# Products over 64 features issued for two heads by turns on the two partition halves

## The chip, the cores and the metric

One core of one Trainium2 chip runs the whole kernel. The metric is the device time in microseconds, the median of three runs. All operands are float32; the large weight products are split into two float32r parts each and done as three products.

## What is computed

Two blocks of a network over 256 tokens of 1024 features. The first block has two layers with a modulation by a condition vector: an even layer (a dilated-mixture attention of 8 heads and a differential attention of 4 heads with two maps each) and an odd layer (banded attention of 16 heads with sinks). The second block has two layers, each with four mixers (stick-breaking attention, an RWKV-7 recurrence, MoBA attention, HGRN2) of 4 heads each and a gated feed-forward part. Every head has 64 features, so the products between queries and keys, and those of the RWKV chunk matrices, contract over 64:

```python
s = jnp.einsum('bhqd,bhkd->bhqk', qs, k) * scale + bias        # attention scores, d = 64
z = jnp.einsum('bhtd,bhsd->bhts', qf[:, :, t0:kv_len], kf[:, :, :kv_len]) * scale   # stick-breaking
S_t = S_{t-1} diag(w_t) + (S_{t-1} a_t) b_t^T + v_t k_t^T ; y_t = S_t r_t           # RWKV, done in chunks of 128
```

## The kernel before

Queries and keys lie feature-major: a tile [128, 2, 256] holds two column tiles of 128 features, which are two heads each, one on partitions 0 to 63 and one on 64 to 127. A product of queries and keys of one head reads one half of the partitions and writes 128 queries by 128 or 256 keys into PSUM. There are two token tiles `t`.

PSUM has two pools of four banks: `mm` for the weight products (`proj_tok`, `proj_fm`, `proj_acc`, lines 237 to 239) and `mx` for everything else: scores (`sc`), values (`pv`), transposes (`pt`, `tr`), the sums of the modulation (`mod`) and all of the mixers' small tiles.

`softmax` (line 358) does the product itself (line 361), then on VectorE the biased minimum (line 363), then on ScalarE the exponential (line 366). It is called once for each head and token tile, so the product of the second token tile, into the same bank, follows in the program behind the VectorE read of the first. The callers are `scores_a` (8 heads, line 611), `scores_b` (4 heads with two maps, line 666), `scores` of the odd layer (16 heads, line 774) and `scores` of `moba` (4 heads, both layers, line 1035). `pipelined` runs the scores of a head two heads (one head of `scores_b`) ahead of its values: transposes (line 375), a copy to SBUF by ScalarE (line 377) and the products with the values (lines 637, 699, 805). In `moba` the scores of head h+1 are a step ahead of the values of head h.

`stick_breaking` (line 958) does for each token tile and each partition half two products of one half into one bank (line 971), then the sigmoid on ScalarE and, two steps later, the other half. `Rwkv.run` makes the chunk matrices (line 1346) for two chunks, two sources and two halves: two products of one half into one bank, then a mask by VectorE (line 1349).

The order on each engine is the planner's: it takes the ready instruction of the highest priority, priority being the program's order, which `lazily(by)` shifts. The odd layer's attention has -3000 and so goes before the weight products around it; the RWKV stream has -4000 against the stream of the other three mixers, with which `weave` mixes it step by step. Weight products fill the rest. The units of weights come by SyncE's queue (line 216), are rounded by ScalarE (line 219) and their rest taken by VectorE (line 220). In the even layer the same queue brings the modulation weights (line 482), which VectorE sums (lines 427 and 429), and the biases (line 381). `later` starts and ends such sums between the heads.

Of the kernel before, what the change touches and what calls it, by code (L numbers as in the profile page):

```python
# [94 lines left out]
NR, NH, NL = 3, 5, 5  # L95
LATE = 300


class Net:
# [109 lines left out]
    def unit(self, src, shape, pieces=1):  # L209
        """[128, 1024] weights: float32 in, split exactly into float32r parts."""  # L210
# [12 lines left out]
    def block(self, w, c0, k0=0, k1=8, pieces=1):  # L223
        """512 columns of w [1024, cols] as units of two k chunks; returns {chunk: (hi, lo)}."""
# [38 lines left out]
    def proj_fm_part(self, act, w, c0, done, k0, k1, ps, cols=4, wb=None):  # L263
        """cols * 128 columns, feature-major: done(i, ps) with ps [128, 2, 256] = column tiles 2i, 2i+1."""
# [43 lines left out]
    def to_T(self, src, t, act, c0, n):  # L308
        """transpose src [128 tokens of tile t, n*128] into chunks c0.. of act (hi, lo)."""
# [13 lines left out]
    def rstd(self, ss, n, eps, m=1):  # L323
        """(ss / n + eps) ** -0.5 for a [128, m] column block."""
# [7 lines left out]
    def norm_stat(self, t, junk):  # L332
        """rstd of token tile t (the squares by halves, times 1/32 squared = 1/D)"""
# [35 lines left out]
    def transpose_p(self, p, dst, evict):  # L369
        """p [128 q, t, 256 keys] -> dst [128 keys, kc, 256 q]"""  # L370
# [26 lines left out]
class Mod:  # L397
    """ada modulation of layer l, on every partition: norm_g * (1 + scale), shift, gate / 2."""

    def __init__(self, n, l):  # L400
        self.n, self.l = n, l
        self.G = n.s2(f"G{l}", tag="mod")
        if l == 0:
            # over the partitions by TensorE, idle as yet
# [43 lines left out]
    def start(self, half, then=None):  # L448
        """scale (first half: on TensorE, idle then) and shift (VectorE), before anything else runs"""
# [43 lines left out]
class AdaNorm:  # L493
    """rms_norm(x) * G + shift, by token tiles, transposed into act"""
# [15 lines left out]
def silu2(n, ps, out):  # L510
    """out = 2 silu(ps)"""
# [16 lines left out]
def pipelined(items, first, second, lag=2, after=None):  # L528
    """first(i) runs `lag` items ahead of second(i)"""
# [10 lines left out]
def pair_out(n, y, sg, col, yT, chunk):  # L540
    """y [128, t, 128] times the gates, into chunk `chunk` of yT"""
# [11 lines left out]
def even_layer(n, mod, later, follow):  # L553
# [24 lines left out]
    # the modulation and the normalized activations by halves of the features, products running along  # L578
# [31 lines left out]
    # dilated attention  # L610
    def scores_a(h):
        b = n.dma_bias(h)
        sp = v2(n.mx("sc"))
        p = v2(n.s2("p", tag="p"))
        rl = n.col(2, "rl")
        b0 = (h % 2) * 64
        for t in range(2):
            l, _ = n.softmax(sp[:, t, :], fm["qa", h // 4][b0:b0 + 64, h // 2 % 2, t * 128:t * 128 + 128],
                             fm["ka", h // 4][b0:b0 + 64, h // 2 % 2, :], b[:, t, :], p[:, t, :])
            nc.vector.reciprocal(rl[:, t:t + 1], l)  # L620
        return p, rl

    ya = {}
    st = {}

    def values_a(h, got):
        p, rl = got
        hh = h % 2
        if hh == 0:
            st["pv"] = n.mx("pv")  # L630
            ya[h // 2] = n.s2("ya", tag="yp").rearrange("p (t d) -> p t d", t=2)
        pv = st["pv"]
        pT = n.s2("pT", tag="pT")
        n.transpose_p(p, pT, nc.scalar.copy)
        for t in range(2):
            for kc in range(2):
                nc.tensor.matmul(pv[:, t * 128 + hh * 64:t * 128 + hh * 64 + 64],
                                 lhsT=pT[:, kc * 256 + t * 128:kc * 256 + t * 128 + 128],
                                 rhs=tok["va", kc][:, h * 64:h * 64 + 64], start=(kc == 0), stop=(kc == 1))
            c = slice(hh * 64, hh * 64 + 64)  # L640
            nc.scalar.activation(ya[h // 2][:, t, c], pv[:, t * 128 + hh * 64:t * 128 + hh * 64 + 64], AF.Copy,
                                 scale=rl[:, t:t + 1])
    pipelined(8, scores_a, values_a, 2, lambda h: later(h // 2) if h % 2 else None)
# [5 lines left out]
    # lambda, on every partition  # L649
# [15 lines left out]
    # differential attention  # L665
    def scores_b(h):
        b = n.dma_bias(8 + h)
        ps_, rs = [], []
        for m in range(2):
            sp = v2(n.mx("sc"))  # L670
            p = v2(n.s2("p", tag="p"))
            b0 = m * 64
            r = n.col(2, "rl")
            for t in range(2):
                l, _ = n.softmax(sp[:, t, :], fm["qb", h // 2][b0:b0 + 64, h % 2, t * 128:t * 128 + 128],
                                 fm["kb", h // 2][b0:b0 + 64, h % 2, :], b[:, t, :], p[:, t, :])
# [47 lines left out]
def odd_layer(n, act, mod, later, follow):  # L724
# [49 lines left out]
    def scores(h):  # L774
        g = h // 4
        b = n.dma_bias(12 + h)
        sp = v2(n.mx("sc"))
        p = v2(n.s2("p", tag="p"))
        den = n.col(4, "den")
        b0 = (h % 2) * 64  # L780
        for t in range(2):
            l, nm = n.softmax(sp[:, t, :], fm["q", h // 4][b0:b0 + 64, (h // 2) % 2, t * 128:t * 128 + 128],
                              fm["k", g % 2][b0:b0 + 64, g // 2, :], b[:, t, :], p[:, t, :],
                              init=sk[:, 16 + h:17 + h])
            nc.scalar.activation(den[:, 2 + t:3 + t], nm, AF.Exp, bias=sk[:, h:h + 1])
            nc.vector.tensor_add(den[:, t:t + 1], den[:, 2 + t:3 + t], l)
        nc.vector.reciprocal(den[:, 0:2], den[:, 0:2])
        return p, den

    yp = {}  # L790
    st = {}

    def values(h, got):
        p, den = got
        hh, g = h % 2, h // 4
        if hh == 0:
            st["pv"] = n.mx("pv")
            yp[h // 2] = n.s2("yc", tag="yp").rearrange("p (t d) -> p t d", t=2)
        pv = st["pv"]
        pT = n.s2("pT", tag="pT")  # L800
        n.transpose_p(p, pT, nc.scalar.copy)
        for t in range(2):
            o = pv[:, t * 128 + hh * 64:t * 128 + hh * 64 + 64]
            for kc in range(2):
                nc.tensor.matmul(o, lhsT=pT[:, kc * 256 + t * 128:kc * 256 + t * 128 + 128],  # L805
                                 rhs=tok[kc][:, g * 64:g * 64 + 64], start=(kc == 0), stop=(kc == 1))
            nc.vector.tensor_scalar(yp[h // 2][:, t, hh * 64:hh * 64 + 64], o, den[:, t:t + 1], None, op0=OP.mult)
# [5 lines left out]
    def after(h):  # L813
        if h in (1, 3, 5):
            later(h // 2)
        if h == 11:
# [10 lines left out]
def first_block(n):  # L827
# [14 lines left out]
    def later(i):  # L842
        """sums of part i; the part before it, complete by now, is spread over the partitions"""
# [12 lines left out]
class PlainNorm:  # L856
    """rms_norm(x) * g, by token tiles, transposed into act"""
# [13 lines left out]
class DoubleNorm:  # L871
    """x := rms_norm(x) * final_g, and the next norm of that, its sum of squares taken from x * final_g"""
# [9 lines left out]
    def tile(self, t):  # L882
# [10 lines left out]
        # 1 / r1^2 = m + eps with m the mean square of x; 1 / (r1 r2)^2 = mean square of y + eps (m + eps)  # L893
# [27 lines left out]
def weave(a, b):  # L921
    """steps of two independent instruction streams, by turns"""
# [7 lines left out]
def zsel(ap, b, z):  # L930
    """[P, m] -> [P, n, b]: every other run of b columns"""
# [3 lines left out]
def zsel4(ap, b, z):  # L935
    """[P, 4 * 128] -> [P, 4, n, b]"""
# [759 lines left out]
```

## Time and profile before

| | us |
|---|---|
| median of three runs | 1361.11 |
| lowest and highest run | 1355.42, 1362.63 |
| span of the profiled execution, first to last instruction | 1352.0 |
| TensorE (PE) busy in it | 1295.5 |
| VectorE (DVE) busy | 843.8 |
| ScalarE (ACT) busy | 647.7 |
| GpSimd (POOL) busy | 71.6 |

The profiled execution gives no time beside its span. Line numbers are those of the kernel before. A float32 matmul of the program stands in the trace as two records (two loads and two matmuls), each of which streams its columns twice. Busy times of PE count matmuls that overlap as one; a matmul's own duration holds its way through the array, so distances between starts or ends tell the pace.

### The profile page before, as it was taken

The page shows a single profiled execution, that of the slowest core. Times are in us where ns is not written, and L with a number is a line of the kernel's source. Part 1 is how long each engine was busy: PE and PEld are TensorE (multiplying, and loading weights), DVE is VectorE, ACT ScalarE, POOL GpSimd, SP SyncE. Part 2 cuts the span into 40 slices and gives each one's busy share as a digit, 9 for nine tenths or more (in the row PEclk, how much of TensorE's full clock was granted, in tenths as well). Part 3 has the DMA queues.
Part 4 walks back from the last instruction along what each step waited for, and adds up shares of the span by engine and source line. Part 5 has one row for each costly group of instructions (what it writes and reads, how often), then busy time and mean ns, then how long its engine had stood idle before and what let it go on. Part 6 is the DMA issues. An engine that isn't in the chain of part 4 may idle for free.

```text
span 1352.0 us, 20294 instructions
## 1 busy us (share of the span) xinstructions
PE 1295.5 (96%) x7824; PEld 1106.9 (82%) x7824; DVE 843.8 (62%) x1438; ACT 647.7 (48%) x1093; POOL 71.6 (5%) x82
## 2 busy tenths in 40 slices
PE   6888988999899999999999999999999999999997
PEld 4767666877798888888899987888888888899986
DVE  6866888656757755576655544657754766755543
ACT  3354645665655335444544443655344444544432
POOL 0111120000001000000000000001000000000000
PEclk8989999999998999999999999999999999999999
DMA  8987865643462323366666655652332465666552
GB/s 313 313 258 243 262 193 173 199 142 111 154 193 80 96 79 110 99 186 187 184 190 187 184 187 159 204 163 79 94 107 66 143 200 171 186 186 179 185 187 90
DMA packets 104956, 227.19 MB, mean 168 GB/s; under 512 B 8206, under 2 KB 8350, under 8 KB 104860
## 3 DMA queue, kind: packets, MB, share of 16 engines
q1 hardware_dynamic: 102560, 219.18, 52.1%
q0 software_dynamic: 1984, 6.60, 1.8%
q8 instruction: 61, 1.00, 0.3%
q14 instruction: 35, 0.29, 0.1%
q10 hardware_dynamic: 316, 0.12, 0.0%
HBM read 224.82 MB, written 1.05 MB: 167 GB/s over the span
## 4 chain that ended last, share of the span: by engine, by line
PE 73%; issue 5%; DVE 5%; DMA 2%; ACT 2%; POOL 1%; POOLq 0%; DVEq 0%; ACTq 0%
PE mm L237 19%; PE mm L239 19%; PE mm L238 19%; PE sc L361 2%; PE p L1378 2%; PE p L1384 1%; PE pv L805 1%; DVE wl L220 1%; ACT wh L219 1%; PE hs L1105 1%; DMA wr<-in_gu_dram 1%; PE cm L1346 1%; PE pt L375 1%; DMA aw<-in_ada_w_dram 1%; PE z L971 1%
## 5 line engine op out<-in xcount | busy, mean ns | idle before, releaser
L220 DVE TENSOR_TENSOR wl<-wr,wh 128x1024 fp32r<-128x1024 f32 (+1 forms) x372 | 432.5, 1168 | 274.9 <-ACT wh L219 272.6
L219 ACT CAST wh<-wr 128x1024 fp32r<-128x1024 f32 (+1 forms) x372 | 369.7, 1002 | 406.3 <-PE mm L239 184.8
L238 PE MATMUL mm<-hl,wh 128*128 128x256 f32 x1104 | 317.3, 288 | 0.0
L237 PE MATMUL mm<-hh,wh 128*128 128x256 f32 x1104 | 315.7, 288 | 1.4 <-ACT hh L320 1.4
L239 PE MATMUL mm<-hh,wl 128*128 128x256 f32 x1104 | 315.4, 286 | 0.0
L237 PEld LDWEIGHTS mm<-hh,wh 128*128 128x128 f32 x1104 | 214.0, 195 | 5.7 <-issue 3.0
L238 PEld LDWEIGHTS mm<-hl,wh 128*128 128x128 f32 x1104 | 214.6, 195 | 2.2 <-issue 1.7
L239 PEld LDWEIGHTS mm<-hh,wl 128*128 128x128 f32 x1104 | 214.5, 194 | 1.3 <-issue 1.2
L237 PE MATMUL mm<-wh,hh 128*128 128x512 f32 (+1 forms) x480 | 190.0, 396 | 0.5 <-ACT hh L320 0.3
L238 PE MATMUL mm<-wl,hh 128*128 128x512 f32 (+1 forms) x480 | 189.6, 395 | 0.4 <-DVE wl L220 0.4
L239 PE MATMUL mm<-wh,hl 128*128 128x512 f32 (+1 forms) x480 | 188.7, 394 | 0.3 <-DVE hl L321 0.3
L237 PEld LDWEIGHTS mm<-wh,hh 128*128 128x128 f32 x480 | 90.6, 189 | 20.0 <-issue 2.5
L238 PEld LDWEIGHTS mm<-wl,hh 128*128 128x128 f32 x480 | 90.7, 189 | 19.3 <-issue 2.2
L239 PEld LDWEIGHTS mm<-wh,hl 128*128 128x128 f32 x480 | 90.5, 189 | 19.1 <-issue 1.2
L237 PE MATMUL mm<-wh,ff 128*128 128x512 f32 x176 | 69.5, 395 | 0.0
L238 PE MATMUL mm<-wl,ff 128*128 128x512 f32 x176 | 69.5, 395 | 0.0
L239 PE MATMUL mm<-wh,ff 128*128 128x512 f32 x176 | 69.4, 395 | 0.0
L429 DVE SCALAR_TENSOR_TENSOR macc<-aw,cs,macc 128x512 f32<-128x512 f32 x78 | 57.8, 755 | 8.0 <-DMA aw<-in_ada_w_dram 7.4
L238 PE MATMUL mm<-wl,yTh 128*128 128x512 f32 x128 | 50.6, 396 | 3.4 <-DVE wl L220 3.4
L239 PE MATMUL mm<-wh,yTl 128*128 128x512 f32 x128 | 50.7, 396 | 0.0
L237 PE MATMUL mm<-wh,yTh 128*128 128x512 f32 x128 | 49.4, 398 | 0.0
L366 ACT ACTIVATE p<-p,nm 128x256 f32<-128x256 f32 (+1 forms) x80 | 39.6, 495 | 19.0 <-DVE nm L363 18.1
(394 smaller groups left out, 1688.4 us busy)
## 6 DMA issues: line engine op xcount, KB each, us to landing
wr<-in_w_in_dram SPq DMA_DIRECT2D x120, 512.0 KB, 3.8
wr<-in_gu_dram SPq DMA_DIRECT2D x88, 512.0 KB, 4.3
wr<-in_w_ffn_down_dram SPq DMA_DIRECT2D x44, 512.0 KB, 3.6
aw<-in_ada_w_dram SPq DMA_DIRECT2D x80, 256.0 KB, 4.0
wr<-in_ab_w_in_dram SPq DMA_DIRECT2D x32, 512.0 KB, 5.3
wr<-in_c_w_in_dram SPq DMA_DIRECT2D x20, 512.0 KB, 4.2
wr<-in_w_branch_dram SPq DMA_DIRECT2D x16, 512.0 KB, 3.4
wr<-in_w_out_dram SPq DMA_DIRECT2D x16, 512.0 KB, 4.3
```

What stands on the lines that cost most here:

```text
L219: nc.scalar.copy(hi[:, i:i + m], raw[:, i:i + m])
L220: nc.vector.tensor_sub(lo[:, i:i + m], raw[:, i:i + m], hi[:, i:i + m].bitcast(F32))
L237: mm(out, lhsT=ah, rhs=bh, start=start, stop=False, **kw)
L238: mm(out, lhsT=ah, rhs=bl, start=False, stop=False, **kw)
L239: mm(out, lhsT=al, rhs=bh, start=False, stop=stop, **kw)
L361: nc.tensor.matmul(ps, lhsT=qT, rhs=kT, start=True, stop=True)
L366: nc.scalar.activation(p, p, AF.Exp, bias=nm, scale=-1.0, accum_out=l)
L375: nc.tensor.transpose(ps[:, kc * 256 + t * 128:kc * 256 + t * 128 + 128], p[:, t, kc * 128:kc * 128 + 128], self.ident)
L429: nc.vector.scalar_tensor_tensor(acc, w, n.cs[:, k:k + 1], acc, op0=OP.mult, op1=OP.add)
L805: nc.tensor.matmul(o, lhsT=pT[:, kc * 256 + t * 128:kc * 256 + t * 128 + 128], rhs=tok[kc][:, g * 64:g * 64 + 64], start=(kc == 0), stop=( ...
L971: nc.tensor.matmul(z[:, i * W:(i + 1) * W], lhsT=q[r, i, t * 128:t * 128 + 128], rhs=k[r, i, 0:W], start=True, stop=True)
L1378: mm(half(p1[c], h), lhsT=aT(c, h), rhs=zsel(X[c][:, hd(h)], z, 0), start=True, stop=True)
```

## The change

A new helper issues the products of a list one after the other, at a priority that puts them ahead of anything that is ready. `softmax` no longer does the product. The four callers take two heads (or the two maps of one head) at a time: they take two banks of `mx`, issue four products by turns on the two partition halves, one half for each bank, and then do the softmaxes of both heads. `pipelined` runs one pair ahead, where it ran two heads ahead. `stick_breaking` issues the four products of a token tile so, and `Rwkv.run` the four of a chunk and source. Docstrings and comments go away besides.

```diff
+HALF = (slice(0, 64), slice(64, 128))
...
+    def products(self, of):
+        with self.lazily(-20000):
+            for out, lhsT, rhs in of:
+                self.nc.tensor.matmul(out, lhsT=lhsT, rhs=rhs, start=True, stop=True)
+
-    def softmax(self, ps, qT, kT, bias, p, init=3.0e38):
+    def softmax(self, ps, bias, p, init=3.0e38):
-        nc.tensor.matmul(ps, lhsT=qT, rhs=kT, start=True, stop=True)
...
+    def scores_a(pr):
+        q, k = fm["qa", pr // 2], fm["ka", pr // 2]
+        sp = [v2(n.mx("sc")) for _ in range(2)]
+        n.products([(sp[hh][:, t, :], q[HALF[hh], pr % 2, t * 128:t * 128 + 128], k[HALF[hh], pr % 2, :])
+                    for t in range(2) for hh in range(2)])
+        for hh in range(2):
+            b = n.dma_bias(pr * 2 + hh)
...
+            for t in range(2):
+                l, _ = n.softmax(sp[hh][:, t, :], b[:, t, :], p[:, t, :])
...
-    pipelined(8, scores_a, values_a, 2, lambda h: later(h // 2) if h % 2 else None)
+    pipelined(4, scores_a, values_a, 1, later)
...
-        pipelined(16, scores, values, 2, after)
+        pipelined(8, scores, values, 1, after)
...
     for t, b in ((0, b0), (1, b1)):
         W = 128 * (t + 1)
+        z = [n.mx("z") for _ in range(2)]
+        n.products([(z[par][:, i * W:(i + 1) * W], q[HALF[par], i, t * 128:t * 128 + 128], k[HALF[par], i, 0:W])
+                    for i in range(2) for par in range(2)])
         for par in range(2):
-            z = n.mx("z")
-            r = slice(par * 64, par * 64 + 64)
-            for i in range(2):
-                nc.tensor.matmul(z[:, i * W:(i + 1) * W], lhsT=q[r, i, t * 128:t * 128 + 128], rhs=k[r, i, 0:W],
-                                 start=True, stop=True)
...
             for store, src, nm in ((ab, bt, "ab"), (ak, kt, "ak")):
+                ps = [n.mx("cm") for _ in range(2)]
+                n.products([(ps[hh][:, p * 256:p * 256 + 256], src[HALF[hh], p, c * 128:c * 128 + 128],
+                             ar[c][HALF[hh], p * 256:p * 256 + 256]) for p in range(2) for hh in range(2)])
                 for hh in range(2):
-                    b0 = hh * 64
-                    ps = n.mx("cm")
-                    for p in range(2):
-                        mm(ps[:, p * 256:p * 256 + 256], lhsT=src[b0:b0 + 64, p, c * 128:c * 128 + 128],
-                           rhs=ar[c][b0:b0 + 64, p * 256:p * 256 + 256], start=True, stop=True)
```

`scores_b`, the odd layer's `scores` and `moba`'s `scores` are changed as `scores_a` is; in `moba` the second pair's scores are issued ahead of the values of head 0, and the loop over the heads has two steps less.

## Rows read from the trace of the kernel before

**Rows 1.** The page's first part: busy time, share of the span, instructions.

```profile
PE 1295.5 (96%) x7824; PEld 1106.9 (82%) x7824; DVE 843.8 (62%) x1438; ACT 647.7 (48%) x1093; POOL 71.6 (5%) x82
```

**Rows 2.** Windows by stage: stretch, length; busy by engine; PE's granted clock, DMA share, GB/s.

```profile
70.00:131.00 61.00, 52.61 (x329) 42.48 (x328) 39.74 (x91) 29.78 (x74) 10.21 (x10) 0.92 0.78 246
131.00:210.00 79.00, 72.60 (x326) 52.27 (x325) 65.82 (x154) 42.50 (x96) 13.63 (x12) 1.00 0.74 228
256.00:325.00 69.00, 68.55 (x418) 51.71 (x416) 41.52 (x167) 44.82 (x133) 1.86 (x4) 1.00 0.43 133
404.00:432.00 28.00, 26.88 (x161) 23.51 (x161) 21.60 (x51) 15.07 (x31) 5.72 (x4) 0.82 0.17 50
524.00:545.00 21.00, 21.00 (x152) 16.95 (x152) 10.02 (x33) 12.93 (x33) 0.00 (x0) 1.00 0.19 54
1019.00:1040.00 21.00, 21.00 (x153) 16.96 (x152) 9.76 (x32) 13.16 (x34) 0.00 (x0) 1.00 0.17 51
```

**Rows 3.** Chain of the odd layer's attention, 256 to 325 us: shares of the stretch.

```profile
by line: PE sc L361 24.1%; PE pv L805 21.2%; PE pt L375 12.9%; PE mm L238 12.2%; PE mm L237 12.0%; PE mm L239 11.5%; PE mod L488 2.8%; issue 1.8%; PE tr L547 1.5%; DVE nm L363 0.4%; DVE p L363 0.1%
```

**Rows 4.** Chain in order of time, from end to end: start us, us, what.

```profile
262.38 0.63 PE sc L361 x4
...
531.38 0.23 PE mm L237
531.61 0.63 PE sc L361 x2
532.24 0.43 PE mm L238
532.66 0.23 PE mm L239
...
535.75 0.41 PE sc L361 x2
```

**Rows 5.** Timeline of PE: start us, us, line, operation, tiles, shape, records.

```profile
390.72 0.28 PE L239 MATMUL mm<-hh,wl 128*128 128x256 f32 x1
390.94 0.48 PE L1194 MATMUL pw<-lw,wa 64*128 64x256 f32 x1
390.95 0.48 PE L1195 MATMUL pa<-shift,wa 64*128 64x256 f32 x1
...
391.70 0.38 PE L1195 MATMUL pa<-shift,wa 64*128 64x256 f32 x1
```

**Rows 6.** Timeline of PE, `moba` of the first mixer layer: first and last run.

```profile
524.36 0.49 PE L361 MATMUL sc<-km,qm 64*128 64x128 f32 x2
...
541.49 0.70 PE L361 MATMUL sc<-km,qm 64*128 64x256 f32 x2
```

**Rows 7.** Chain, chunk matrices of the first mixer layer.

```profile
432.49 2.97 PE cm L1346 x16
...
439.36 1.80 PE cm L1346 x7
...
441.42 1.24 PE cm L1346 x8
```

**Rows 8.** Timeline of PE, stick-breaking of the second mixer layer: first, fifth, last run.

```profile
901.43 0.48 PE L971 MATMUL z<-sbqk 64*128 64x128 f32 x2
...
913.27 1.13 PE L971 MATMUL z<-sbqk 64*128 64x256 f32 x4
...
917.34 0.70 PE L971 MATMUL z<-sbqk 64*128 64x256 f32 x2
```

**Rows 9.** Timeline of PE, the even layer's scores: first and last run of `scores_a`, of `scores_b`.

```profile
70.66 0.70 PE L361 MATMUL sc<-ka,qa 64*128 64x256 f32 x4
...
100.79 0.70 PE L361 MATMUL sc<-ka,qa 64*128 64x256 f32 x2
...
131.57 1.92 PE L361 MATMUL sc<-kb,qb 64*128 64x256 f32 x10 [0.28 <-ACT kb L563]
...
179.40 0.70 PE L361 MATMUL sc<-kb,qb 64*128 64x256 f32 x2
```

**Rows 10.** Timeline of PE at its longest stand in the even layer (in brackets: idle before).

```profile
114.67 1.85 PE L488 MATMUL mod<-macc,cst 128*128 128x512 f32 x2 [4.64 <-POOL macc L484]
```

More of the change, by code (lines that the diff above doesn't have):

```diff
@@ L608, in even_layer @@
     yT = n.pair("yT")
[L611 to L621, printed above, removed]
@@ L623, in even_layer @@
-    ya = {}
[L624 to L642, printed above, removed]
@@ new lines, in even_layer, with values_a @@
+    ya = {}
+    def values_a(pr, got):
+        pv = n.mx("pv")
+        ya[pr] = n.s2("ya", tag="yp").rearrange("p (t d) -> p t d", t=2)
+        for hh, (p, rl) in enumerate(got):
+            h = pr * 2 + hh
+            pT = n.s2("pT", tag="pT")
+            n.transpose_p(p, pT, nc.scalar.copy)
+            for t in range(2):
+                for kc in range(2):
+                    nc.tensor.matmul(pv[:, t * 128 + hh * 64:t * 128 + hh * 64 + 64],
+                                     lhsT=pT[:, kc * 256 + t * 128:kc * 256 + t * 128 + 128],
+                                     rhs=tok["va", kc][:, h * 64:h * 64 + 64], start=(kc == 0), stop=(kc == 1))
+                c = slice(hh * 64, hh * 64 + 64)
+                nc.scalar.activation(ya[pr][:, t, c], pv[:, t * 128 + hh * 64:t * 128 + hh * 64 + 64], AF.Copy,
+                                     scale=rl[:, t:t + 1])
@@ L772, in odd_layer @@
     n.proj_fm(act, w, 512, q_done(1))
[L774 to L788, printed above, removed]
@@ L790, in odd_layer, with scores @@
-    yp = {}
[L791 to L807, printed above, removed]
+    def scores(pr):
+        g = pr // 2
+        q, k = fm["q", pr // 2], fm["k", g % 2]
+        sp = [v2(n.mx("sc")) for _ in range(2)]
+        n.products([(sp[hh][:, t, :], q[HALF[hh], pr % 2, t * 128:t * 128 + 128], k[HALF[hh], g // 2, :])
+                    for t in range(2) for hh in range(2)])
+        got = []
+        for hh in range(2):
+            h = pr * 2 + hh
+            b = n.dma_bias(12 + h)
+            p = v2(n.s2("p", tag="p"))
+            den = n.col(4, "den")
+            for t in range(2):
+                l, nm = n.softmax(sp[hh][:, t, :], b[:, t, :], p[:, t, :], init=sk[:, 16 + h:17 + h])
+                nc.scalar.activation(den[:, 2 + t:3 + t], nm, AF.Exp, bias=sk[:, h:h + 1])
+                nc.vector.tensor_add(den[:, t:t + 1], den[:, 2 + t:3 + t], l)
+            nc.vector.reciprocal(den[:, 0:2], den[:, 0:2])
+            got.append((p, den))
+        return got
@@ new lines, in odd_layer, with values @@
+    yp = {}
+    def values(pr, got):
+        g = pr // 2
+        pv = n.mx("pv")
+        yp[pr] = n.s2("yc", tag="yp").rearrange("p (t d) -> p t d", t=2)
+        for hh, (p, den) in enumerate(got):
+            pT = n.s2("pT", tag="pT")
+            n.transpose_p(p, pT, nc.scalar.copy)
+            for t in range(2):
+                o = pv[:, t * 128 + hh * 64:t * 128 + hh * 64 + 64]
+                for kc in range(2):
+                    nc.tensor.matmul(o, lhsT=pT[:, kc * 256 + t * 128:kc * 256 + t * 128 + 128],
+                                     rhs=tok[kc][:, g * 64:g * 64 + 64], start=(kc == 0), stop=(kc == 1))
+                nc.vector.tensor_scalar(yp[pr][:, t, hh * 64:hh * 64 + 64], o, den[:, t:t + 1], None, op0=OP.mult)
@@ L811, in gated, with after @@
             pair_out(n, yp[blk * 4 + pr], [sg[blk, 0], sg[blk, 1]], pr * 128, yT, blk * 4 + pr)
[L813 to L816, printed above, removed]
+    def after(pr):
+        if pr < 3:
+            later(pr)
+        if pr == 5:
             gated(0)
@@ L1033, in moba, with scores @@
     got = {}
[L1035 to L1045 removed]
+    def scores(pr):
+        sp = [n.mx("sc") for _ in range(2)]
+        n.products([(sp[hh][:, t * 128:t * 256 + 128], q[HALF[hh], pr, t * 128:t * 128 + 128],
+                     k[HALF[hh], pr, 0:128 * (t + 1)]) for t in range(2) for hh in range(2)])
+        for hh in range(2):
+            h = pr * 2 + hh
+            p = n.s2("p", tag="tm")
+            for t in range(2):
+                W = 128 * (t + 1)
+                o = t * 128
+                l, _ = n.softmax(sp[hh][:, o:o + W], n.cst[:, C_ZC + 256 - W:C_ZC + 256], p[:, o:o + W])
+                nc.vector.reciprocal(rl[:, t * 4 + h:t * 4 + h + 1], l)
+            got[h] = p
     scores(0)
@@ L1049, in moba @@
     for h in range(4):
-        if h < 3:
-            scores(h + 1)
+        if h == 0:
+            scores(1)
             yield
```

30 lines of the change are left out of this document (13 added, 17 removed).

## The prediction

> **What bounds the kernel now.** I read the page's busy times first: PE is busy for 96% of the span, the next engine, DVE, for 62% [rows 1]. An average over stages hides where PE is not the limit, so I cut the span at the stages that the change touches and read the windows [rows 2]. The reader is to see three kinds. In the odd layer's attention (256 to 325 us) PE is busy 68.55 of 69 us, ACT 44.8 and DVE 41.5; in `moba` of either mixer layer PE is busy the whole 21 us and DVE about 10. There PE is the limit. In the even layer (70 to 210 us) PE stands still for 8.4 of 61 and 6.4 of 79 us, DVE is busy 65.8 of the 79, and the DMA queues are about three quarters full. In the stick-breaking stretch (404 to 432 us) PE is busy 26.88 of 28, but at a mean clock of 0.82, with DVE at 21.6.
>
> Then the chain of waits in the odd layer [rows 3]: nothing but PE's own lines carries weight, and the largest is the score product with 24.1% of 69 us, 16.6 us. DVE and ACT together are under 1%. What shortens PE's work here shortens the stage, as long as another engine does not step in.
>
> Last, the pace of single products, from the chain's pieces, which run from end to end [rows 4]. A product of 128 queries and 256 keys over 64 features is two records and takes 0.63 us alone; with 128 keys it takes 0.41. The weight product right behind it takes 0.43 where the others of its line take 0.23. So a change from 128 rows to 64 and back costs 0.20 us beside the product, and one lone product 0.83. In the same rows stands a piece with four records, two products of two heads that the planner happened to put side by side, and it takes 0.63 too. Two heads on two halves run at once, for the price of one.
>
> The kernel already has one place that goes by turns between the halves, into two banks: the two low-rank products at lines 1194 and 1195 [rows 5]. Starts of a pair lie 0.01 us apart, and eight records (four products of 256 columns) go from the end of the weight product before, 390.72 + 0.28 = 391.00, to 391.70 + 0.38 = 392.08. That is 1.08 us, with the switch 1.28, for what costs 4 x 0.83 = 3.32 as four lone products. This is the new order, measured.
>
> **The change part by part.** The number of products and their columns stays. What changes is how often PE goes over to 64 rows, and how many go at once. After the change there are 32 groups of four: 4 in `scores_a`, 4 in `scores_b`, 8 in the odd layer, and over both mixer layers 4 in stick-breaking, 8 in the chunk matrices and 4 in `moba`.
>
> Odd layer: 32 products stand in 25 runs now (the timeline of line 361), 16.6 us and 25 x 0.20 = 5.0 of switches, 21.6. Eight groups cost 8 x 1.28 = 10.2. Saved: **11.4**. PE is the limit there; ACT would be at 44.8 of 58 us, so all of it is counted.
>
> `moba`: each layer has seven runs [rows 6], three of 128 keys and four of 256: 3 x 0.41 + 4 x 0.63 + 7 x 0.20 = 5.2. Two groups of one pair at 128 and one at 256 keys: no row shows one; it lies between a lone pair of 256 keys (0.83) and a full group (1.28), and being the mean of both in records I take 1.05. Saved 5.2 - 2.1 = 3.1, in both layers **6.1** (bounds 5.2 to 7.0), all on PE's path.
>
> Chunk matrices: three runs in the first layer [rows 7], 2.97 + 1.80 + 1.24 = 6.0 and 0.6 of switches, 6.6; the second layer alike, 13.2 in all. The planner has mixed the halves here already, so less is left. Eight groups alone cost 10.2; if two groups stand side by side, a further pair of records costs 0.22 (the distance of starts in the group above), so 1.28 + 4 x 0.22 = 2.16 for two, 8.6 in all. Saved 3.0 to 4.6; I take **4.0**, nearer the second, as both sources are ready together.
>
> Stick-breaking: in the second layer seven runs [rows 8]. The timeline counts them from their start, 0.07 more than the chain from end to end (0.70 there is 0.63 here): four of 0.41, one of 1.06 (two products of one half) and two of 0.63, 4.0 in all, and 1.4 of switches: 5.4. After: a group at 128 keys, which no row shows (between a lone product's 0.61 with its switch and a full group's 1.28; each half has the columns of a lone product of 256 keys, so I take 0.85), and a full one: 2.1. Saved 3.3, both layers 6.6. But the stretch also hangs on the RWKV stream's steps over DVE and POOL, so PE's relief may turn into idle time. Bounds 0 and 6.6; I take half, **3.3**.
>
> Even layer: `scores_a` has 15 runs, `scores_b` 10, of which the first holds ten records [rows 9]. 15 x 0.83 = 12.5 becomes 4 x 1.28 = 5.1; 1.9 + 9 x 0.63 + 10 x 0.20 = 9.6 becomes 5.1. PE has 11.9 us less. But it stands for 14.8 of the 140 us already [rows 2], once for 4.64 at a sum of the modulation that POOL has not finished [rows 10], and DVE, which sums the modulation and splits the weights, is at 83% in the second half. That work does not shrink, so relief becomes idle time for the most part. Bounds 0 and 11.9; I take **4.0**, nearer to nothing by the DVE share.
>
> The rest I cost at nothing. The VectorE read of the first token tile no longer stands between the two products of a head, which frees DVE's start and costs the first read at most the 0.45 us by which the group is longer than one product; other heads' reads and PE's weight products cover that. The biases still are two DMAs for two heads on SyncE's queue, now issued together; the three bias buffers free at the same reads as before, and what is queued behind them there are the same weights. `later` follows the values of a pair as now, so the modulation's DMAs and POOL's sums keep their place. In `moba` the second pair's scores move ahead of head 0's values, which takes DVE and ACT work forward in a stretch where both are half idle [rows 2]. The new order waits for two banks instead of one: behind a product that waits stand, on PE, the weight products, and for those the whole kernel. That is the third rival.
>
> The sum: 11.4 + 6.1 + 4.0 + 3.3 + 4.0 = 28.8 us. The profiled span of 1352.0 becomes 1323.2. The median of the runs is 9.1 above that span, so 1361.1 becomes **1332.3**. All bounds high: 11.4 + 7.0 + 4.6 + 6.6 + 11.9 = 41.5, or 1319.6.
>
> **The rivals.** First, the evictions pace the attention. Each pair passes from PE to DVE to ACT to PE to ACT to PE to DVE, all through four banks, and two of these are now held at once. If that loop, and not PE's work, takes the 69 / 8 = 8.6 us for a pair in the odd layer, the stage keeps its length and the even layer too: 28.8 - 11.4 - 4.0 = 13.4 saved, **1347.7**. For it: DVE at 83% in 131 to 210 us. Against it: in the odd layer ACT is at 65% and DVE at 60%, and the chain hardly touches them. The Trainium skill's page "TensorEngine Tiling (Array Packing)", section "PSUM Bottleneck", says that tiling speeds up TensorE but not the emptying of PSUM, which may then be the limit; by that rule the time is this rival's, and by the row on the odd layer's chain it is not.
>
> Second, the groups do not come out by turns. A bank that frees late parts the two halves, and each group becomes two runs of two products of one half. One of these costs 1.06 (the stick-breaking run of four records), 1.26 with its switch, so a group 2.5 instead of 1.28. 32 x 1.24 = 40 would be more than the gain; in the odd layer 8 x 2.5 = 20 against 21.6 now, in `moba` and stick-breaking 2 us, the chunk matrices nothing. About 4 us in all, **1357**. Against it: the priority holds the four together as soon as both banks are there, and pairs formed in places even without it [rows 4].
>
> Third, slower. PE takes its queue in order, and the products go ahead of everything that the planner thinks ready. If a bank comes free later on the chip than in the plan, PE stands at the product with the weight products behind it, as at the modulation's sum for 4.64 us [rows 10]. The place is the four banks of `mx`, most of all where the RWKV stream and the others share them. It decides from 28.8 / 32 = 0.9 us of standing for a group on the average; at 1.5 us it gives 1361.1 + 32 x 0.6 = **1380**. Against it: now there are 32 places of two banks where there were over 70 runs that each could stand.
>
> PE's clock is a side case of all. It was at 0.82 in the stick-breaking stretch, at half speed for 0.18 x 2 x 28 = 10 us, some 5 us lost [rows 2]; in the second layer it was not. One more or one less such stretch moves the time by 5 us either way.
>
> **How the numbers follow.** Forecast 1332 with its own range of 1319 to 1344: 64%. Evictions 18%, not by turns 10%, slower 8%. The range of 8 in 10 takes in the forecast, its upper bound of 41.5 with some of the clock's 5 us, and the first rival with the same: 1316 to 1352. Within 0.5%, about what a measurement of this kernel can tell from no change, is 1354.3 to 1367.9: the second rival and a little of the first, 11%. Slower by more: 7%. Faster by more: 82%.
>
> **What would show it.** In the changed kernel's timeline the score products stand in 16 runs of eight records in both layers of the first block, pairs 0.01 us apart, each group 1.08 from end to end; 8 in the odd layer, with the next piece of the chain still PE. The stretch from the odd layer's first score to its last values is 11 us shorter, `moba` 3 in each layer. Wrong would be: runs of four records with starts 0.22 apart (second rival), the odd layer as long as now with PE idle (first), or new waits of score products for DVE or ACT of over 0.9 us each (third).

## The result and the profile after

| | before | after |
|---|---|---|
| median, us | 1361.87 | 1338.34 |
| ratio, 95% interval | | 0.9864 (0.9825 to 0.9902) |
| span of the profiled execution, us | 1352.0 | 1338.4 |

The change makes the kernel faster by 1.4%; forecast was 1332, with 1316 to 1352 around it. Beside the later experiments the changed kernel took 1338.71 and the kernel before 1352.81, a ratio of 0.9874 (0.9839 to 0.9909); the quotient of these two medians alone is 0.9896. The kernel before spreads more than the changed one, from 1346 to 1369 us, and its long executions are those with a low mean granted clock (1347.7 us at 0.991, 1363.95 at 0.973); executions of the changed kernel all have 0.984 to 0.990. So the first median of before is the high one, and about 14 us is what the change is worth between executions of the same clock (those of the kernel before at 0.984 to 0.990 have a median of 1352.2).

The changed kernel's page, first part, answers [rows 1]; its windows by stage answer [rows 2] (columns as there; the first window is the even layer's first attention, the third the odd layer's, then stick-breaking in layer 0, then `moba` of both layers).

```profile
PE 1275.9 (95%) x7824; PEld 1101.6 (82%) x7824; DVE 843.1 (63%) x1438; ACT 647.6 (48%) x1093; POOL 66.2 (5%) x82
```

```profile
68.20:130.50 62.30, 53.66 (x351) 46.27 (x352) 43.38 (x95) 31.75 (x76) 10.26 (x11) 0.92 0.83 266
130.50:210.00 79.50, 72.18 (x338) 55.28 (x339) 69.33 (x158) 42.89 (x100) 11.17 (x12) 0.98 0.73 234
252.60:315.00 62.40, 61.34 (x417) 50.84 (x417) 40.16 (x166) 44.86 (x132) 2.66 (x5) 1.00 0.46 142
394.56:418.85 24.29, 21.50 (x161) 18.92 (x161) 22.07 (x52) 16.39 (x32) 5.59 (x4) 1.00 0.22 68
511.00:533.00 22.00, 22.00 (x156) 18.41 (x154) 8.15 (x31) 12.99 (x34) 0.00 (x0) 1.00 0.18 59
1006.80:1028.70 21.90, 21.90 (x155) 18.41 (x154) 8.13 (x31) 12.99 (x34) 0.00 (x0) 1.00 0.17 60
```

PE is busy 19.6 us less (17.1 in a second profile of the changed kernel, with 1278.4). The relief lies in the odd layer (68.55 busy of 69 us before, 61.34 of 62.4 now) and around stick-breaking; `moba` is PE from end to end as before, and from its first score to the state's first product it takes 21.9 us where it took 19.5.

The chain of the odd layer (252.6 to 315 us), by line, answers [rows 3]: the scores fall from 24.1% of 69 us to 14.1% of 62.4, and DVE and ACT now have 6.5%.

```profile
by line: PE pv L815 25.5%; PE sc L364 14.1%; PE mm L240 12.6%; PE mm L239 12.5%; PE mm L238 12.4%; PE pt L382 11.9%; PE mod L495 2.8%; DVE wl L221 2.0%; ACT wh L220 1.7%; DVE p L370 1.5%; PE tr L554 1.4%; ACT p L373 1.0%; DVE yc L817 0.3%; 
```

The changed kernel's timeline of PE, line of the products (start us, us, line, tiles, shape, records), answers [rows 6 to 9]: even layer, odd layer, stick-breaking, chunk matrices, `moba`.

```profile
68.21 1.14 PE L364 MATMUL sc<-ka,qa 64*128 64x256 f32 x8 [0.48 <-ACT ka L570]
74.88 1.33 PE L364 MATMUL sc<-ka,qa 64*128 64x256 f32 x4 [2.82 <-DVE nm L370]
...
252.61 2.00 PE L364 MATMUL sc<-kd,q 64*128 64x256 f32 x16
266.47 1.14 PE L364 MATMUL sc<-kd,q 64*128 64x256 f32 x8
284.42 1.13 PE L364 MATMUL sc<-kd,q 64*128 64x256 f32 x4
286.07 1.13 PE L364 MATMUL sc<-kd,q 64*128 64x256 f32 x4
...
394.56 0.72 PE L364 MATMUL z<-sbqk 64*128 64x128 f32 x8
...
425.39 1.90 PE L364 MATMUL cm<-ar,kk 64*128 64x256 f32 x8
428.51 1.14 PE L364 MATMUL cm<-ar,shift 64*128 64x256 f32 x8
...
513.54 0.92 PE L364 MATMUL sc<-km,qm 64*128 64x128 f32 x4
515.95 0.92 PE L364 MATMUL sc<-km,qm 64*128 64x128 f32 x4
```

Eight records in 1.14 us are a whole group, two halves at once; four records in 1.13 are one half alone, at the price of a whole group. In the odd layer six of eight groups are whole and two are parted (284 to 293 us), in the even layer seven of eight are whole, in `moba` the second pair is parted in both layers, and of the chunk matrices one group in layer 0 takes 1.90 us, eight records of which the second half's four come behind the first half's.

### The profile page after: what moved, and what is told of

Same layout as the page of the kernel before. It is cut to its first block, busy times and chain, and to the rows that moved or that the text cites. A ratio compares the mean times of both kernels' runs of the same rounds, so it can differ in the third digit from the quotient of the medians.

```text
span 1338.4 us, 20297 instructions
## 1 busy us (share of the span) xinstructions
PE 1275.9 (95%) x7824; PEld 1101.6 (82%) x7824; DVE 843.1 (63%) x1438; ACT 647.6 (48%) x1093; POOL 66.2 (5%) x82
## 4 chain that ended last, share of the span: by engine, by line
PE 69%; DVE 9%; issue 5%; DMA 3%; ACT 2%; POOL 1%; DVEq 0%; POOLq 0%; ACTq 0%; SPq 0%
PE mm L240 19%; PE mm L239 19%; PE mm L238 19%; DVE wl L221 2%; PE p L1386 2%; PE p L1392 2%; DMA aw<-in_ada_w_dram 1%; PE sc L364 1%; PE pv L815 1%; ACT wh L220 1%; DMA wr<-in_gu_dram 1%; PE hs L1115 1%; PE cm L364 1%; DVE macc L436 1%; DMA wr<-in_ab_w_out_dram 1%
```

## The experiments

Medians and ratios to the kernel before, each against executions of before on the same chip:

| kernel | us | ratio (95%) |
|---|---|---|
| changed, again | 1338.71 | 0.9874 (0.9839 to 0.9909) |
| half after half | 1345.43 | 0.9926 (0.9898 to 0.9955) |
| no priority | 1343.48 | 0.9907 (0.9871 to 0.9943) |
| state products together | 1331.78 | 0.9821 (0.9786 to 0.9855) |
| `moba` as before | 1334.86 | 0.9842 (0.9807 to 0.9877) |
| odd layer as before | 1343.95 | 0.9912 (0.9872 to 0.9952) |
| even layer as before | 1342.85 | 0.9905 (0.9870 to 0.9940) |
| both mends | 1329.65 | 0.9820 (0.9784 to 0.9856) |
| stick-breaking as before | 1342.75 | 0.9916 (0.9882 to 0.9950) |
| chunk matrices as before | 1338.60 | 0.9885 (0.9852 to 0.9918) |
| both mends, chunk matrices as before | 1332.12 | 0.9839 (0.9802 to 0.9875) |
| odd layer alone | 1347.67 | 0.9946 (0.9916 to 0.9976) |

The intervals are about 5 us either way, for the most part from the spread of the kernel before. A difference of 4 us between two rows is therefore not clear by the ratios alone, and the windows beside it have to bear it.

The changed kernel was timed once more, as the base of the others.

> The changed kernel as it is, timed beside the following three on the same chip, so that a few us between them can be told: 1336 to 1340, some 15 us below the kernel before as it runs beside it.

### Is it the turns?

```diff
-            for out, lhsT, rhs in of:
+            for out, lhsT, rhs in of[0::2] + of[1::2]:
                 self.nc.tensor.matmul(out, lhsT=lhsT, rhs=rhs, start=True, stop=True)
```

> The changed kernel with one edit: each group of four products goes out half after half (two of one half, then two of the other) where the changed kernel goes by turns; grouping, banks and priority stay. Theory 1, the gain is that two halves stream at once: a full group by turns takes 1.06 us from its first start to the next instruction's, eight records of one pace would take 1.93, so 0.86 more for each of some 18 groups that come out whole (6 odd layer, 7 even layer, 2 stick-breaking, 3 chunk matrices) and half of that for the small ones; PE busy rises by 14 to 18 us, the odd layer's attention by 5, and the time goes from 1338 to 1350 to 1356. Rival 2, the gain is the grouping (fewer changes between 128 and 64 rows, no product behind a VectorE read): then the order inside a group does nothing and the time stays within 3 us of 1338.

Theory 1 fell. In this kernel's timeline of the odd layer a whole group takes as long as by turns:

```profile
269.48 1.14 PE L364 MATMUL sc<-kd,q 64*128 64x256 f32 x8
...
287.90 1.13 PE L364 MATMUL sc<-kd,q 64*128 64x256 f32 x4
289.88 1.13 PE L364 MATMUL sc<-kd,q 64*128 64x256 f32 x4
```

By the single records the second half's products start 0.01 us behind the first half's, though they stand two places later in the queue. So the prediction's "PE takes its queue in order" does not hold between the two halves: the third product of the queue starts 0.5 us before the second. PE's busy time is 1278.3 us, and 1278.4 in the second run of the changed kernel. What pays is that the four stand together; the order among them does not change PE's busy time. The rival's 3 us is not right either: the time is 6.7 us above the changed kernel. It is idle time of PE: span less busy is 65.4 us, in the changed kernel's two profiles 62.5 and 57.8, and up to the odd layer's first score PE stands idle for 39.0 us against 35.0 and 33.5. Why that order makes PE wait more was not settled.

### Is it the priority?

```diff
-        with self.lazily(-20000):
-            for out, lhsT, rhs in of:
-                self.nc.tensor.matmul(out, lhsT=lhsT, rhs=rhs, start=True, stop=True)
+        for out, lhsT, rhs in of:
+            self.nc.tensor.matmul(out, lhsT=lhsT, rhs=rhs, start=True, stop=True)
```

> The changed kernel with one edit: the products keep the priority of the code around them, the extra -20000 is gone; they stand in the program in the same order, by turns. Theory 1, the priority holds the four together, as the prediction said: without it the odd layer's 9 runs of products become about 15 (the program order leaves single products), stick-breaking's first groups part into pairs; 6 more runs of 0.2 us of change and some 6 pairs that lose their partner at 0.3 to 0.6 each give 4 to 8 us, 1342 to 1346. Rival, the planner would place them so anyway since the pair is issued at once: within 2 us of 1338.

1343.48, 4.8 us above the changed kernel: theory 1 by the time, and the odd layer has 15 runs of products instead of 9. The mechanism is not shown. This run's profile is of its shortest execution (1339.69), and in it PE is busy for 1278.1 us, no more than in the changed kernel, and the odd layer takes 129.1 us from its first score to the RWKV stream's first product, where the changed kernel's two profiles have 128.2 and 129.4. By the medians the priority is a third of the gain; where it lies stays open.

### The parts, put back one at a time

Each kernel has one part as in the kernel before, the rest changed: for the odd layer head after head again, with the product inside the softmax.

```diff
-    def scores(pr):
-        sp = [v2(n.mx("sc")) for _ in range(2)]
-        n.products([...])
+    def scores(h):
+        sp = v2(n.mx("sc"))
...
-        pipelined(8, scores, values, 1, after)
+        pipelined(16, scores, values, 2, after)
```

> The changed kernel with the odd layer's scores and values as in the kernel before (head after head, two heads ahead); the rest changed. Theory 1: the odd layer's part is what the stage shows, 134.7 us from its first score to the RWKV's first product before and 128.2 after, so the time is 6.5 us above the changed kernel's, 1344 to 1346. Rival, the term of the prediction: 11.4 above, 1349 to 1350, the difference having been taken by another stage that the order of work in the odd layer reaches (the weights that it fetches ahead). Second rival: the relief moves to the next stage as waiting for weights, under 3 above.

> The odd layer's attention as in the changed kernel, everything else (even layer, stick-breaking, chunk matrices, moba) as in the kernel before. Putting parts back one at a time gave 4.1 (even), 5.2 (odd), 4.0 (stick-breaking), -0.1 (chunk matrices) and -3.8 (moba), 9.4 in all, where the whole change is worth 14.1. Theory 1: the odd layer alone is worth what its stage shows, 134.7 to 128.2 or a little more, 5 to 7 below the kernel before, which runs at 1352 to 1353: 1346 to 1348; the rest of the 4.7 is not in this layer. Rival, the prediction's term is there when nothing else is changed: 11.4 below, 1341.

From the odd layer's first score to the RWKV stream's first product, in one window each: the changed kernel (again), the one with the odd layer put back, the one with the odd layer alone.

```profile
251.04:380.41 129.37, 124.90 (x791) 105.63 (x791) 85.71 (x237) 82.28 (x195) 6.01 (x8) 0.99 0.51 155
```

```profile
251.48:387.58 136.10, 132.12 (x792) 106.60 (x791) 87.07 (x237) 82.06 (x195) 6.01 (x8) 0.99 0.48 147
```

```profile
257.31:386.66 129.35, 124.88 (x791) 105.58 (x790) 85.69 (x237) 82.25 (x195) 6.01 (x8) 0.99 0.51 156
```

The stage is 6.7 us longer with the part put back, the time 5.2; alone the part is worth 5.5 (1353.16 to 1347.67), with 129.4 us for the stage where the kernel before has 134.7. Both runs say theory 1; the 11.4 of the prediction is in neither.

The even layer's two attentions were put back in the same way.

> The changed kernel with the even layer's two attentions as in the kernel before; the rest changed. Theory 1: PE is relieved of 8 to 12 us there, but most of it becomes idle time under VectorE and the modulation's DMAs, so the time is 3 to 5 us above the changed kernel's, 1341 to 1343. Rival: nothing of it reaches the end, within 1.5 us. Second rival: all of it does, 8 or more above.

4.1 us above the changed kernel: theory 1 by the time. The windows from the first score to the odd layer's first score, of the changed kernel (again) and of this one:

```profile
67.56:251.04 183.48, 165.74 (x948) 137.19 (x948) 142.97 (x291) 98.02 (x208) 23.21 (x26) 0.95 0.74 234
```

```profile
70.77:255.31 184.54, 169.06 (x926) 133.96 (x925) 137.71 (x287) 96.44 (x206) 26.40 (x25) 0.95 0.71 223
```

PE is busy 3.3 us less although 22 more matmuls stand in the window (the first score comes 3.2 us earlier, ahead of weight products), and stands idle for 17.7 us instead of 15.5. Counted from the start of the span, where both have the same 1204 matmuls, PE is busy 217.6 us against 225.0 and idle 33.5 against 30.4. So PE is relieved of 7.4 us, a little less than theory 1's 8 to 12, and 3.1 of them become idle time: not most of it.

For stick-breaking and the chunk matrices the loop takes one bank and issues two products of one half, without the priority.

> The changed kernel with stick-breaking's products as in the kernel before (half after half, each into one bank when its turn comes); the rest changed. The stage from the first z product to the first chunk matrix is 24.3 us in layer 0 and 28.0 in layer 1; before it was 27.7 (with PE's clock at 0.82) and 28.9. Theory 1, the part is worth about 1 us a layer and the rest of layer 0's difference was the clock: 25.3 and 28.9, the time 2 us above the changed kernel's 1338.7. Rival, the prediction's middle value of 3.3 over both layers or its bound of 6.6: 1342 to 1345. Second rival: it hangs on the RWKV stream, no change.

4.0 us by the medians, near the prediction's 3.3 and not theory 1's 2; but not by PE's work. Windows of the kernel before in layer 0, first two, and of the changed kernel over the same steps, last two:

```profile
404.70:411.90 7.20, 6.08 (x40) 4.80 (x40) 3.83 (x12) 1.46 (x4) 2.50 (x2) 1.00 0.40 128
411.90:422.10 10.20, 10.20 (x43) 8.88 (x41) 7.36 (x25) 5.41 (x13) 0.00 (x0) 0.50 0.00 0
```

```profile
394.56:401.80 7.24, 5.34 (x43) 4.31 (x43) 5.02 (x15) 3.31 (x6) 2.37 (x2) 1.00 0.35 115
401.80:412.00 10.20, 9.76 (x81) 9.59 (x82) 10.20 (x29) 7.28 (x17) 0.00 (x0) 1.00 0.01 2
```

Before, PE goes on at 1.2 GHz (granted 0.50) for 10.2 us and does 43 matmuls; in the changed kernel it stays at 2.4 and does 81 in the same time, and DVE is the one that never rests. The stage from the first `z` product to the first chunk matrix, before (layer 0, layer 1), in this run (layer 0) and in the changed kernel (layer 1; its layer 0 is the window 394.56:418.85 further up):

```profile
404.71:432.42 27.71, 26.59 (x156) 23.06 (x156) 21.24 (x51) 14.84 (x30) 5.72 (x4) 0.82 0.17 51
901.43:930.32 28.89, 27.92 (x175) 22.64 (x175) 23.52 (x56) 17.07 (x34) 6.33 (x4) 1.00 0.23 67
```

```profile
393.24:420.86 27.62, 25.50 (x157) 21.32 (x157) 20.58 (x51) 15.52 (x31) 5.73 (x4) 0.88 0.14 39
```

```profile
889.09:917.05 27.96, 25.91 (x179) 21.51 (x179) 23.55 (x56) 16.73 (x34) 5.48 (x4) 1.00 0.27 86
```

The three profiles with the old stick-breaking have a mean clock of 0.82 (before), 0.88 (this run) and 0.77 (odd layer alone) in layer 0's stage, of 27.6 to 29.3 us. Of the eleven profiles with the new form ten have 1.00 there, and 24.3 to 24.4 us; the one without the priority has 0.93, and 24.9. In layer 1, at full clock in both, the stage takes 28.9 us with the old form and 28.0 with the new (two of the eleven, the changed kernel's second profile among them, have 0.94 there, and 28.9). So the part is worth 0.9 us where the clock stays and 3.3 to 5.0 where the old form lets it fall. It need not fall in each execution: this run's seven go from 1338.0 to 1347.3 us, and the profiled one, 1345.8, is one of the long ones.

> The changed kernel with the chunk matrices as in the kernel before (half after half in the program, without the priority); the rest changed. Theory 1: the planner mixes the halves there by itself, the part is worth nothing or costs 0.3 us a layer (first chunk matrix to moba's first score 92.2 us in layer 0 and 89.8 in layer 1, before 91.9 and 89.5): 1338 to 1339. Rival, the prediction's term: 2 us a layer, 1342 to 1343.

1338.60 against 1338.71: the part is worth nothing, theory 1. Timeline of PE in this run (layer 1; old form):

```profile
912.51 1.29 PE L1356 MATMUL cm<-ar,kk 64*128 64x256 f32 x8
914.42 1.13 PE L1356 MATMUL cm<-ar,shift 64*128 64x256 f32 x4 [0.62 <-DVE ab L1359]
```

The old form's first eight records come at two halves' pace without any help: the program issues them half after half, an order which *Is it the turns?* showed to run at once too. The half that stands alone behind them has waited 0.62 us for a bank that VectorE's mask (`ab`) had to empty. The changed kernel has the same wait in layer 0 (0.35 us, DVE `ab`) and 2.97 us for its first sixteen records, as before [rows 7].

### Where moba's gain went

```diff
             if c == 0:
                 pst = n.mx("pst")
-                for h in range(4):
+                with n.lazily(-20000):
+                    for h in range(4):
...
```

> The changed kernel with one edit: the eight products of the RWKV state (tile pst, 64 output columns at one half of the output partitions) get the priority -20000, so that they go out in one piece as they did in the kernel before; in the changed kernel they alternate one by one with the products of tiles pr and py. Theory 1, that alternation is where moba's saving went: in the stretch of moba pst cost 1.93 us where it cost 0.66 before, pr 0.4 more, so 1.6 to 2.0 us a layer come back, 3 to 4 in all, 1334 to 1335. Rival, PE is waiting for the RWKV stream there and the alternation fills idle time: no change, 1338.

The changed kernel's timeline of PE behind `moba` in layer 0 (`pst` writes 64 columns of the array, the others 128), and then this run's:

```profile
533.01 0.33 PE L1428 MATMUL pst<-R,bk 128*64 128x64 f32 x2
533.27 0.43 PE L1440 MATMUL py<-R,ab 128*128 128x64 f32 x2
533.54 0.39 PE L1442 MATMUL py<-vt,ak 128*128 128x64 f32 x2
...
535.60 0.33 PE L1428 MATMUL pst<-R,bk 128*64 128x64 f32 x2
535.86 0.43 PE L1410 MATMUL pr<-vt,ak 128*128 128x64 f32 x2
536.22 0.33 PE L1429 MATMUL pst<-vt,bk 128*64 128x64 f32 x2
536.48 0.43 PE L1410 MATMUL pr<-vt,ak 128*128 128x64 f32 x2
```

```profile
532.87 0.34 PE L1429 MATMUL pst<-R,bk 128*64 128x64 f32 x4
533.03 0.29 PE L1431 MATMUL pst<-vt,bk 128*64 128x64 f32 x4
533.15 0.34 PE L1429 MATMUL pst<-R,bk 128*64 128x64 f32 x4
533.27 0.33 PE L1431 MATMUL pst<-vt,bk 128*64 128x64 f32 x4
533.53 0.43 PE L1443 MATMUL py<-R,ab 128*128 128x64 f32 x2
```

Together all eight take 0.66 us; one by one each `pst` with its neighbour takes 0.62 (535.60 to 536.22), where a neighbour alone takes 0.22 to 0.27. Two things are lost with the block. PE changes between 64 and 128 columns at each product, and a `pst` has no partner: in the block the products for the two halves of the output partitions start 0.01 us apart by the single records, two at once, as the two halves of the features do in a score group. The time falls to 1331.78, 6.9 us below the changed kernel. From `moba`'s first score to layer 1's first RWKV product it is 361.0 us where the changed kernel's two profiles have 364.2 and 362.9, and in layer 1 up to the end 328.6 against 331.6 and 330.4. Theory 1 in its cause; its 1.6 to 2.0 a layer is the lower end of what the profiles show, 1.7 to 3.2, and its 3 to 4 in all is about half of what the time shows.

> The changed kernel with moba as in the kernel before (head after head, seven single runs a layer); all other parts changed. Theory 1: moba's change saves 1.6 us a layer at its products (not 3.1, since its second pair comes out half after half), and costs as much again because its loop has two steps fewer, which shifts the RWKV steps woven with it and makes the state products alternate with others; so without it pst stands together again and the time is within 1.5 us of 1338. Rival A, moba saves the predicted 3 a layer and something else was lost: 1344. Rival B, moba's change is a loss throughout: 1335.

1334.86, below the changed kernel by 3.9: rival B. With the old form of `moba` the eight `pst` products stand together (their starts lie within 0.51 us, with one other matmul between; in the changed kernel within 5.3 us, with 25). So the alternation comes with the new form. It does not come from the groups' priority: the kernel without the priority alternates in the same way. What is left is the loop, which has two steps fewer and with which the RWKV steps are woven one for one; no run changes the number of steps alone. `moba`'s part, meant to save, costs 3.9 us by the medians.

```diff
-    def products(self, of):
-        with self.lazily(-20000):
+    def products(self, of, by=-20000):
+        with self.lazily(by):
...
-                     k[HALF[hh], pr, 0:128 * (t + 1)]) for t in range(2) for hh in range(2)])
+                     k[HALF[hh], pr, 0:128 * (t + 1)]) for t in range(2) for hh in range(2)], by=-500)
```

and the `pst` edit with it:

> The changed kernel with two edits: the RWKV state's products go out in one piece (priority -20000), and moba's groups get the priority -500 in place of -20000, with which the second pair waits for two banks and comes out by turns, not half after half with other work between. Theory 1: 3.1 us a layer from the state's products as measured, and in moba two runs of 0.85 us and their change of 0.2 become one group of about 1.05, 0.8 us a layer: 7 to 8 us below the changed kernel, 1330 to 1331. Rival: the second pair's later start holds the values of head 0 back and eats the 0.8: as with the first edit alone, 1332.

1329.65, 9.1 us below the changed kernel and the fastest of all, but the time does not tell theory 1 from its rival: the ratio is 0.9820, with the first edit alone 0.9821. The profiles are for theory 1, with 360.5 us from `moba`'s first score to layer 1's first RWKV product and 326.9 in layer 1 up to the end, where the first edit alone has 361.0 and 328.6. Timeline of `moba` in it:

```profile
508.11 0.49 PE L364 MATMUL sc<-km,qm 64*128 64x128 f32 x4
510.46 1.52 PE L364 MATMUL sc<-km,qm 64*128 64x256 f32 x12
```

At -500 the second pair waits until the first pair's 256-key products go, and the twelve records take 1.45 us to the next instruction's start, where the changed kernel pays 0.63 + 0.85 + 0.85.

> The kernel with both mends (the RWKV state's products in one piece, moba's groups at -500), and the chunk matrices as in the kernel before. By theory 1 on the chunk matrices 0 to 0.6 us below the kernel with both mends: 1329 to 1330. Rival: 4 above, 1333 to 1334.

1332.12, 2.5 above: neither figure. The chunk matrices' part may be worth something once the rest is mended; the two intervals overlap.

## Why the prediction was right, and where its terms were not

The time lies in the range, and direction and mechanism hold: PE was the limit, and two halves at once are worth what the rows said. But the 28.8 us did not come: 23.5 between the first medians, 13.6 between the profiled spans, 14.1 beside the experiments, about half of the sum. That 1332.3 lies only 6 us from the measured 1338.3 is in part luck (see the base, below). Term by term:

**Unit prices.** They hold. A whole group measures 1.06 from its start to the next instruction's, at 128 keys 0.65, so 0.85 with the switch, which the prediction took for a group that no row showed; two groups side by side 1.93, with the switch 2.13 (2.16 in the prediction).

**Odd layer**, 11.4: the stage gained 6.6, the time 5.2 to 5.5. From the starts of all records, products and the changes before and behind them take 21.9 us before (the prediction: 21.6) and 12.2 after (10.2): 9.7 of the 11.4 came. The difference is chiefly the second rival in two of eight pairs, four runs of 1.26 for two of 1.28, 2.5 us. The step that failed is "so all of it is counted": of the 9.7 some 3 come back, 0.6 as idle time (transposes wait 1.0 us for ACT) and the rest inside PE's other lines: from start to start the scores take 17.0 us before and 10.7 after, and all other products of the stretch, which should have lost the changes beside the scores, 52.0 and 51.9. Weight products are now followed directly by a transpose or a value product 27 times where it was 21; what that costs was not measured, and the remainder stays open.

**`moba`**, 6.1: minus 3.9. The first pair came in two runs (0.42 and 0.63 us) and the second half after half (0.85 each), so the new runs cost 3.6 us a layer with four changes, not 2.1. What failed beside that is "The rest I cost at nothing". It asked what DVE and ACT do in the stretch, and not what the RWKV stream does that is woven with it; the state's products were moved, and no step had them.

**Chunk matrices**, 4.0: nothing. The rows had it (16 records in 2.97 us, both sources): in the kernel before both halves run at once already, and the prediction said that less is left, but it assumed that two groups come whole, with banks for both. They don't: the first sixteen records still take 2.97 us, and one group 1.90. From start to start the runs of both layers add up to 12.5 us in five runs before and 11.1 in seven after, with 0.20 for each run 13.5 and 12.5: 1.0 us of the 4.0. That the banks which VectorE's mask empties pace them, the first rival in its small form, is likely and not shown throughout: each of the two profiles, changed and old form, has one such wait, of 0.35 and 0.62 us. The Trainium skill's page "TensorEngine Tiling (Array Packing)", section "PSUM Bottleneck", which stood beside that rival, says that emptying PSUM may become the limit after a fourfold speedup of TensorE. The wait for `ab` agrees with it here at a twofold one; in the odd layer, where VectorE's read of the scores has 1.5% of the chain, it did not decide.

**Stick-breaking**, 3.3 between 0 and 6.6: 4.0 measured, right in size by luck, through a side case. The working had PE's work at 5.4 before and 2.1 after, and its relief perhaps as idle time. It did become idle time (PE rests 2.8 us of 24.3, DVE 2.2), and layer 1 gained 0.9. Layer 0 gained 3.4, most of it since the old form ran 10.2 us of its stage at 1.2 GHz; the clock stood in the prediction as 5 us either way, and it belonged to this term.

**Even layer**, 4.0 between 0 and 11.9: the odd layer's first score comes 3.6 us earlier, and putting the part back costs 4.1. The figure is right, the way to it only in part: the working had 11.9 us of relief, most of it lost as idle time. PE was relieved of 7.4 (put back) or 4.9 (first profiles), and 3.1 or 1.3 of that became idle time. Less relief than assumed, and a smaller share of it lost, offset each other; that is luck. Some of the missing relief can be the clock, whose mean up to the odd layer's first score is 0.94 in the changed kernel's two profiles, 0.95 with the part put back and 0.96 before. The third rival's wait is in the trace (2.82 us at the second group, for DVE `nm`), but once only, and the kernel before has one of 2.1 us for the same.

**The base.** "The median of the runs is 9.1 above that span" was added as a constant. A time is 1.7 to 1.9 us above its own span in every execution; the rest was that the three runs and the profile lay at different points of a spread that follows the clock. With 1.75 on the span of 1352.0 the forecast would have come out at 1325, too low by 13; the high base hid half of what the terms had too much. The five parts put back sum to 9.5 us, less than the 14.1 of the whole; each has an interval of some 5 us either way, so what the remainder is stays open.

## What to carry to other kernels

Products over 64 rows are worth putting side by side on both halves, and for PE's work it is enough that the four stand together in the queue with both banks free; a half that goes alone costs as much as both. In `moba` it was waiting for both banks that made the second pair whole. The order inside a group did not change PE's work here, though half after half was 6.7 us slower for a reason that stayed open. Before costing a moved step at nothing, list what is woven with it by the step and which narrow products could end up between wide ones. Take the mean clock of the profiled execution beside those of the others before a difference between span and median is added to a forecast.

## What was not expected of the hardware

- Two products on one half followed in the queue by two on the other run at once as four by turns do: 1.071 us for eight records against 1.064, starts 0.01 us apart. With sixteen records in one go it is 2.03 against 1.93 in the even layer.
- Products with 64 output columns lose much between others with 128: a `pst` product takes 0.08 us in its block of eight, but one with a neighbour of 0.22 takes 0.62, which is 0.32 more. That is the change there and back and the lost partner together; no run parts the two.
- In a stretch where PE was busy for 6.08 of 7.20 us it then worked at 1.2 GHz for 10.2 us; in the changed kernel, busy for 5.34 of 7.24, it kept 2.4 GHz, and ten of eleven profiles with that form of stick-breaking kept it through the stage. Why, these runs don't tell.
